# Layer 0's mixers in another order of steps, with other PSUM tiles, and the heads' norm as a product with a matrix of ones

## The chip, the core and the metric

The kernel runs on one core of a Trainium2 chip. The core has five engines with queues of their own that run at the same time: TensorE (PE: matrix products; PEld is its weight loading, which overlaps the products), VectorE (DVE), ScalarE (ACT), GpSimd (POOL) and SyncE (SP), which issues the loads of weights. Each engine takes its instructions in the order in which they stand in its queue; an instruction that has to wait for another engine holds back everything behind it. TensorE writes its results into PSUM, which has eight banks of 128 partitions by 512 fp32 numbers, and ScalarE or VectorE read them from there; a bank can be written again only when its readers are done. The metric is the device time of one execution in microseconds (us).

## What is computed (cut)

Two blocks on 512 positions of width 1024. Layer 0 of the first block has a mixer of two parts, a gated linear attention with four heads (GLA) and a sparse attention with eight heads (NSA); behind it come feed-forward layers, a spatial gating unit and a second block, which the change does not touch. Of layer 0's mixer:

```python
def _gla(q, k, v, g_lr, r, w_gate, b_gate, norm_g):
    glog = log_sigmoid(g_lr @ w_gate + b_gate) / 16          # the decays, (512, 4 heads x 64)
    b = cumsum of glog within chunks of 64 positions
    q_t, k_t, k_end = qc * exp(b), kc * exp(-b), kc * exp(b_last - b)
    a = where(causal, q_t @ k_t.T, 0)                        # within a chunk
    S_t = exp(b_last) * S_(t-1) + k_end.T @ v                # from chunk to chunk
    o = a @ v + q_t @ S_prev
    o = o * rsqrt(mean(o * o, axis=-1) + 1e-6) * norm_g      # each head's norm, over its 128 features
    return o * silu(r)

def _nsa(q, kc, vc, ks, vs, kw, vw, gate_logits, ...):
    k_cmp, v_cmp = compress(kc), compress(vc)                # 31 blocks of the 512 positions
    p_c = masked_softmax(q @ k_cmp.T);  o_c = p_c @ v_cmp
    # here every block is selected and the window is the whole sequence: both are causal attention
    o_s = masked_softmax(q @ ks.T) @ vs
    o_w = masked_softmax(q @ kw.T) @ vw
    return g0 * o_c + g1 * o_s + g2 * o_w

m = concatenate([_gla(...), _nsa(...)]) @ w_out
```

## The kernel before, in words

Matrix products with weights are done in split precision. `unit` loads 128x1024 weights (`wraw`), ScalarE rounds them to `whi` (line 272) and VectorE takes the rest `wlo` (line 273); `split` does the same with activations (lines 280 and 281). `mm3` then makes three products (lines 286 to 288). So one projection of 512 positions and 1024 inputs is 24 products with 512 columns each; here it is called a projection.

Layer 0's mixer is not written as one loop. Its parts are generators, and a string, `SEQUENCE`, is walked letter by letter: each letter takes the next step of a part. The letters are:

- `A`: scores of one head and branch (`sn`, `halves`: q k for four blocks of 128 queries, causal mask added by a product), their row maximum on VectorE (`mx`, line 934), exponentials with row sums on ScalarE (`pn`, line 936), and the division and gate on GpSimd (line 941). There are 16 such steps (8 heads, 2 branches).
- `T`: the 10 transposes of these probabilities (`pt`, `halves`, line 960) and their split into `pth` and `ptl` (lines 280 and 281).
- `P`: the products with the values (`on`, line 975); after every second one VectorE adds the result into `ob` (line 983).
- `c`: the compressed scores and softmax of one block of 128 queries (`sc`, line 873; lines 877 to 891), four steps.
- `C`: the transposes of the compressed probabilities (`ptc`, line 898), their split, and the products with the compressed values (`oc`, lines 286 to 288), copied to `ob` by ScalarE (line 905).
- `g`: the next step of the GLA part, in the order of `steps` in `gla`: two projections `gk`, the decays, two projections `gq`, and then `decayed` and the four projections `gv` by turns, `states`, and four projections `gr`. `decays` is a small transpose (`glrp`), a copy (`glrT`), two products (`zg`), and for each of two halves a log sigmoid and a running sum (lines 1007 to 1011 and 1054). `decayed` makes `e1` and from it the end-decayed keys, transposes these (`ktp`, line 1067) and scales `gq` and `gk`.
- `0` to `3`: the four GLA heads, four steps each: `atp`, `gop`, then the norm (`gsum`, `grc`, `cbg`), and the product with the gate (`goh`). `s`: the splits of `ob`.

A scheduler places the instructions of these steps on each engine near the place where the letters stand, not exactly there. PSUM banks are tiles with tags: in layer 0 tag `g` has two banks and serves projections, `sc`, `ptc`, `oc`, `glrp`, `zg`, `ktp` and the heads; tags `x` and `y` have one bank each and serve the transposes of `T` and, ahead of them, `kcp` and `vcp` (the compressed keys and values, line 803); `a`, `b` and `c` serve the scores; `o` the values.

After layer 0's mixer the output projection starts (`l`, `first_half("eo", ...)`), which reads the heads and `ob` from `cat`.

The program of the kernel before around the change:

Of the kernel before, what the change touches and what calls it, by code (L numbers as in the profile page):

```python
# [10 lines left out]
F32 = mybir.dt.float32  # L11
# [3 lines left out]
AF = mybir.ActivationFunctionType  # L15
# [4 lines left out]
P = 128  # L20
T = 512
NT = 4
# [3 lines left out]
EPS = 1e-6  # L26
# [180 lines left out]
for _k, _v in VEC_SIZES.items():  # L207
# [6 lines left out]

SEQUENCE = ("Acgc Acgcg CT AgTgP ATgP AgTP AgTgP ATgP ATgP AgTPg ATgP0 A0TgP0 AT1P1 ATgP12 AT2P2 ATgP03 A1T3Ps2 sT3P s3Ps"
            .replace(" ", ""))

RINGS = (("raw", 3), ("hi", 4), ("lo", 4)), (("raw", 2), ("hi", 2), ("lo", 2))  # L220
# [17 lines left out]
class Kernel:  # L238
# [395 lines left out]
    def run(self):  # L634
        tc, nc, a = self.tc, self.nc, self.a
        with ExitStack() as ctx:
            def pool(name, bufs=1, **kw):
                return ctx.enter_context(tc.tile_pool(name=name, bufs=bufs, **kw))

            cp = pool("const")  # L640
            self.small = pool("small", 2)
            self.rbp = pool("rbp", 1)
            self.rings = {r: [pool("w" + r, n)] * n for r, n in RINGS[0]}
            self.A = pool("A", 2)

            nc.scalar.preload_act_table_set("natural_log_exp_and_others")
            self.vecs = cp.tile([P, NVEC], F32, name="vecs")
            nc.scalar.dma_start(self.vecs, a["vecs"][:, :NVEC])
            self.consts = cp.tile([P, NCONST], F32, name="consts")
            self.coff = self.a["coff"]  # L650
            self.ident = self.cst("ident")
            self.ones = cp.tile([P, P], F32, name="ones")
            nc.vector.memset(self.ones, 1.0)
            self.mhalf = cp.tile([P, NT], F32, name="mhalf")
            nc.vector.memset(self.mhalf, -0.5)
            self.identb = cp.tile([P, P], BF, name="identb")
            self.causb = cp.tile([P, P], BF, name="causb")
            self.mod = cp.tile([P, 48], F32, name="mod")

            cat = self.layer0_mix()  # L660
            self.ps = pool("ps", 2, space=PSUM, reuse_waits="tile")
            self.pbufs = {"g": 2, "o": 2, "s": 4}
            self.wide = True
            for r, n in RINGS[1]:
                self.rings[r] = self.rings[r] + [pool(f"w{r}2", n, reuse_waits="tile")] * n
            self.hp = pool("hp", reuse_waits="tile")
            self.mp = pool("mp", reuse_waits="tile")
            self.B = pool("B", 2, reuse_waits="tile")
            self.rows = pool("rows", reuse_waits="tile")
            self.h = self.hp.tile([P, NT, D], F32, name="h")  # L670
            nc.scalar.dma_start(self.h, a["x"])
            st, evac = self.norm_evac(self.tokens(), "ng01", False)
            tail = self.first_half("eo", cat, evac)
            tail, st = self.ffn(0, tail, st)
            tail, st = self.sgu(tail, st)
            tail, st = self.ffn(1, tail, st)
            tail, st = self.mixer2(tail, st)
            self.swiglu(tail, st)
            assert self.pos == len(self.plan)


    def layer0_mix(self):
        tc, nc, a = self.tc, self.nc, self.a
        with ExitStack() as ctx:
# [4 lines left out]
            nb = ctx.enter_context(tc.tile_pool(name="nsa", bufs=1))  # L689
# [121 lines left out]
            gb = ctx.enter_context(tc.tile_pool(name="gla", bufs=1, reuse_waits="tile"))  # L811
            gw = ctx.enter_context(tc.tile_pool(name="glw", bufs=2, reuse_waits="tile"))
            gla, heads = self.gla(x, col, rb, ntm, gb, gw)
            parts = dict(zip("cCATP", self.nsa_attention(qs, khh, klo, ntm, vhl, kc, vcmp, nb, wk, ob)))
            parts["g"] = gla
            parts.update(zip("0123", heads))

# [30 lines left out]
    def nsa_attention(self, qs, khh, klo, ntm, vhl, kc, vcmp, nb, wk, ob):  # L848
# [13 lines left out]
        def compressed():  # L862

            for i in range(NT):
                p = split_parts[i % 2]()[:, :256].bitcast(F32)
                pcs.append(p)
                p = p.rearrange("p (h c) -> p h c", h=8)
                neg = self.cst("cneg").rearrange("p (t c) -> p t c", t=NT)[:, i]
                msk = self.cst("cmask").rearrange("p (t c) -> p t c", t=NT)[:, i]
                for g in range(2):  # L870
                    s = self.bank(self.ps, "sc", "g")
                    for j in range(4):
                        nc.tensor.matmul(s[:, j * 64:(j + 1) * 64], qs[:, g, j, i * P:(i + 1) * P], kc[g], start=True, stop=True)

                    sp = s[:, :256].rearrange("p (h e c) -> p h e c", h=4, e=2)
                    pg = p[:, 4 * g:4 * g + 4]
                    nc.vector.tensor_tensor(pg, sp[:, :, 0], neg.unsqueeze(1).to_broadcast([P, 4, 32]), ALU.add)
                    nc.vector.tensor_tensor(pg, pg, sp[:, :, 1], ALU.add)
                mx = st.tile([P, 8], F32, tag="cmx", name="cmx", bufs=2)
                nc.vector.tensor_reduce(mx, p, AX.X, ALU.max)  # L880
                nc.gpsimd.tensor_tensor(p, p, mx.unsqueeze(2).to_broadcast([P, 8, 32]), ALU.subtract)
                nc.scalar.activation(p, p, AF.Exp)
                if i == 0:

                    nc.vector.tensor_tensor(p, p, msk.unsqueeze(1).to_broadcast([P, 8, 32]), ALU.mult)
                sm = st.tile([P, 8], F32, tag="csm", name="csm", bufs=2)
                nc.vector.tensor_reduce(sm, p, AX.X, ALU.add)
                nc.vector.tensor_scalar_max(sm, sm, 1e-30)
                nc.vector.reciprocal(sm, sm)
                nc.vector.tensor_tensor(sm, sm, g3[:, i, :, 0], ALU.mult)  # L890
                nc.gpsimd.tensor_tensor(p, p, sm.unsqueeze(2).to_broadcast([P, 8, 32]), ALU.mult)
                yield

        def compressed_values():
            for g in range(2):
                pt = self.bank(self.ps, "ptc", "g")
                for i in range(NT):
                    nc.tensor.transpose(pt[:, i * P:(i + 1) * P], pcs[i][:, g * P:(g + 1) * P], self.ident)
                ph, pl = (t() for t in split_parts)
                self.split(ph, pl, pt)  # L900
                v = [t[:, g].rearrange("p h d -> p (h d)") for t in vcmp]
                for e in range(2):
                    o = self.bank(self.ps, "oc", "g")
                    self.mm3(o, tuple(t[:, e * P:(e + 1) * P] for t in v), (ph, pl), True, True)
                    nc.scalar.copy(ob[:, 2 * g + e], o)
            yield

# [41 lines left out]
        def transpose_steps():  # L949
            for k in todo:  # L950
                ps = probs.pop(k)
                parts[k] = []
                for e, kbs in enumerate(((0,), (1, 3), (2,))):
                    n = 256 if e == 2 else T
                    pt = self.bank(self.ps, f"pt{e}_", "xy"[e]) if e < 2 else halves[:, 1]
                    for kb in kbs:
                        c0 = place[kb][1]
                        for i in range(kb, NT):
                            c = c0 + (i - kb) * P
                            nc.tensor.transpose(pt[:, c:c + P], ps[i][:, kb * P:(kb + 1) * P], self.ident)  # L960
                    ph, pl = (t() for t in split_parts)
                    self.split(ph[:, :n], pl[:, :n], pt)
                    parts[k].append((ph, pl))
                yield
# [18 lines left out]
                        nc.vector.tensor_tensor(t, t, o[half * 64:half * 64 + 64], ALU.add)  # L983
                yield

        return compressed(), compressed_values(), score_steps(), transpose_steps(), value_steps()

    def pv(self, o, p, nk, wk, v, eng, pt):

# [23 lines left out]
    def gla(self, x, col, rb, ntm, gb, wk):  # L1013
# [78 lines left out]
        def steps():  # L1092
            for i in range(2):
                nc.vector.tensor_mul(gk[:, i], self.fm("gk", x), rb)
                yield
            decays()
            yield
            queries(0)
            yield
            queries(1)  # L1100
            yield
            gv.append(gb.tile([P, NT, T], F32, tag="gv", name="gv"))
            tm = self.tm("gv", x, (2, 2, 2, 2), 512, pairs=((0,), (1,), (2,), (3,)))
# [24 lines left out]
        def head(h):  # L1128
# [17 lines left out]
            sq = wk.tile([P, T], F32, tag="a", name="gsq", bufs=1)  # L1146
            nc.scalar.activation(sq, o, AF.Square)
            yield
            gs = self.bank(self.ps, "gsum", "g")
            for c in range(NT):  # L1150
                nc.tensor.matmul(gs[:, c:c + 1], sq[:, c * P:(c + 1) * P], self.ones[:, 0:1],
                                 start=True, stop=True)
            rc = self.small.tile([P, NT], F32, tag="rcol4", name="grc", bufs=4)
            self.pow_half(rc, gs[:, :4], 1.0 / 128.0, EPS)
            yield
            o = self.bank(self.ps, "cbg", "g")
            self.col_to_bc(o, rc)
            t = wk.tile([P, T], F32, tag="b", name="goh")
            nc.vector.tensor_mul(t, g, o)
            if self.cat is None:  # L1160
                self.cat = self.pair(self.A)
            self.split(self.cat[0][:, h], self.cat[1][:, h], t)
# [695 lines left out]
```

## Time and profile before

| | |
|---|---|
| median of three runs | 2034.1 us (2033.73 to 2039.08) |
| the profiled execution, its own time | 2034.54 us |
| its span from first to last instruction | 2032.7 us |
| TensorE busy over the span | 97% |
| VectorE, ScalarE, GpSimd busy | 68%, 43%, 22% |
| layer 0's mixer, to its last product with values | about the first 271 us of the span |

TensorE is the busy engine of the whole, so time is saved where TensorE waits, where its granted clock is low, or where it has less to do. The places below are given in us from the start of the span.

### The profile page before, as it was taken

How to read it: one execution, taken by the hardware profiler on the slowest of the kernel's cores; microseconds unless marked ns; L12 is line 12 of the kernel's file. 1: busy time of each engine (PE TensorE's matmuls, PEld its weight loads, DVE VectorE, ACT ScalarE, POOL GpSimd, SP SyncE). 2: the span in 40 equal slices, each digit the busy share in tenths (PEclk: the TensorE clock that was granted, in tenths of full speed). 3: DMA queues.
4: the chain of work that ended last, by engine and by line, in shares of the span. 5: the costliest groups of instructions: out<-in, count | busy, mean ns of one | idle time of the engine just before them, and what ended most of it. 6: DMA issues, size and time to landing. Idle time of an engine off the chain costs nothing.

```text
span 2032.7 us, 26315 instructions
## 1 busy us (share of the span) xinstructions
PE 1981.8 (97%) x10120; PEld 1674.6 (82%) x10120; DVE 1385.0 (68%) x1896; ACT 882.4 (43%) x1466; POOL 454.2 (22%) x349
## 2 busy tenths in 40 slices
PE   8989999999999899999999999999999999999997
PEld 6867889888888788888988888898888889888885
DVE  7676555799995758886688996633563655545964
ACT  5445555544344434224634443434755333532432
POOL 3222223433402100003344330200000002222306
PEclk9989999999999999999999999999999999999998
DMA  7311132323331746652233333132122223323231
GB/s 253 89 32 43 42 135 91 107 83 114 104 115 62 277 154 193 204 182 79 94 94 104 104 113 109 61 103 73 61 72 67 83 94 94 104 73 125 84 94 42
DMA packets 60589, 213.56 MB, mean 105 GB/s; under 512 B 6951, under 2 KB 8296, under 8 KB 60080
## 3 DMA queue, kind: packets, MB, share of 16 engines
q1 hardware_dynamic: 57888, 203.89, 31.0%
q0 software_dynamic: 1328, 4.23, 0.7%
q10 hardware_dynamic: 1248, 3.76, 0.6%
q8 instruction: 80, 1.31, 0.3%
q14 instruction: 45, 0.37, 0.1%
HBM read 206.59 MB, written 2.10 MB: 103 GB/s over the span
## 4 chain that ended last, share of the span: by engine, by line
PE 82%; DVE 7%; issue 5%; POOL 4%; ACT 1%; DMA 0%; SPq 0%; POOLq 0%; ACTq 0%; DVEq 0%
PE g L286 12%; PE g L288 12%; PE g L287 12%; PE a L286 6%; PE a L287 6%; PE a L288 6%; PE t L286 2%; PE t L288 2%; PE t L287 2%; PE h L287 2%; PE h L288 2%; PE h L286 2%; PE l L286 2%; PE l L288 2%; PE l L287 2%
## 5 line engine op out<-in xcount | busy, mean ns | idle before, releaser
L273 DVE TENSOR_TENSOR wlo<-wraw,whi 128x1024 fp32r<-128x1024 f32 (+1 forms) x310 | 445.9, 1442 | 183.3 <-ACT whi L272 180.1
L272 ACT CAST whi<-wraw 128x1024 fp32r<-128x1024 f32 (+1 forms) x310 | 323.5, 1045 | 403.8 <-PE g L287 203.8
L286 PE MATMUL g<-a,whi 128*128 128x512 f32 x1200 | 473.7, 395 | 0.0
L288 PE MATMUL g<-a,wlo 128*128 128x512 f32 x1200 | 470.0, 392 | 0.0
L287 PE MATMUL g<-a,whi 128*128 128x512 f32 x1200 | 469.8, 391 | 0.0
L288 PEld LDWEIGHTS g<-a,wlo 128*128 128x128 f32 x1200 | 225.9, 188 | 46.8
L286 PEld LDWEIGHTS g<-a,whi 128*128 128x128 f32 x1200 | 226.3, 189 | 45.8 <-DVE a L1614 0.2
L287 PEld LDWEIGHTS g<-a,whi 128*128 128x128 f32 x1200 | 226.3, 189 | 45.0
L286 PE MATMUL a<-whi,a 128*128 128x512 f32 x624 | 243.3, 390 | 0.0
L288 PE MATMUL a<-whi,a 128*128 128x512 f32 x624 | 242.8, 389 | 0.0
L287 PE MATMUL a<-wlo,a 128*128 128x512 f32 x624 | 242.8, 389 | 0.0
L286 PEld LDWEIGHTS a<-whi,a 128*128 128x128 f32 x624 | 117.2, 188 | 24.5 <-DVE a L1768 0.2
L288 PEld LDWEIGHTS a<-whi,a 128*128 128x128 f32 x624 | 117.1, 188 | 24.5
L287 PEld LDWEIGHTS a<-wlo,a 128*128 128x128 f32 x624 | 117.2, 188 | 23.9
L273 DVE TENSOR_TENSOR wlo<-wt,whi 128x1024 fp32r<-128x1024 f32 x64 | 101.7, 1588 | 32.6 <-ACT whi L272 30.9
L1755 POOL TENSOR_TENSOR wt<-wraw,wraw 128x1024 f32<-128x1024 f32 x32 | 99.0, 3095 | 95.3 <-DMA wraw<-wbig 95.3
L561 POOL TENSOR_TENSOR mg<-a,rowng 128x512 f32<-128x512 f32 x28 | 38.7, 1388 | 342.6 <-DVE a L553 340.1
L286 PE MATMUL h<-a,whi 128*128 128x256 f32 x384 | 108.7, 286 | 2.0 <-ACT a L555 0.9
L280 ACT CAST a<-yt 128x512 fp32r<-128x512 f32 x64 | 39.9, 623 | 161.6 <-POOL yt L1755 117.1
L287 PE MATMUL h<-a,whi 128*128 128x256 f32 x384 | 108.4, 283 | 1.5 <-DVE a L614 1.5
L288 PE MATMUL h<-a,wlo 128*128 128x256 f32 x384 | 107.9, 283 | 0.0
L272 ACT CAST whi<-wt 128x1024 fp32r<-128x1024 f32 x64 | 67.1, 1048 | 72.2 <-PE g L287 60.5
(431 smaller groups left out, 3526.7 us busy)
## 6 DMA issues: line engine op xcount, KB each, us to landing
wraw<-wbig SPq DMA_DIRECT2D x320, 512.0 KB, 3.7
wada<-wada SPq DMA_DIRECT2D x48, 512.0 KB, 3.5
cw<-cmp_w SPq DMA_DIRECT2D x2, 1024.0 KB, 10.4
rowng<-rows POOLq DMA_DIRECT2D x4, 512.0 KB, 5.8
h<-x ACTq DMA_DIRECT2D x1, 2048.0 KB, 10.2
out<-a SPq DMA_DIRECT2D x8, 256.0 KB, 2.2
xin<-xT SPq DMA_DIRECT2D x3, 512.0 KB, 7.9
qt<-qt ACTq DMA_DIRECT2D x12, 128.0 KB, 2.3
```

The costliest lines, as they stand in the source:

```text
L272: self.nc.scalar.copy(hi, raw)
L273: self.nc.vector.tensor_tensor(lo, raw, hi.bitcast(F32), ALU.subtract)
L280: self.nc.scalar.copy(hi, src)
L286: mm(out, s[0], m[0], start=start, stop=False)
L287: mm(out, s[0], m[1], start=False, stop=False)
L288: self.gemm = mm(out, s[1], m[0], start=False, stop=stop).ins
L561: nc.gpsimd.tensor_tensor(mg[c], t, g[:, c * 512:c * 512 + 512], ALU.mult)
L1755: nc.gpsimd.tensor_tensor(t, a, b, op)
```

## The change

The order of the steps is another one, `C` is cut into two steps (`C` now stands for the transposes and their split, `D` for the products with the compressed values), the compressed scores and the transposes of the compressed probabilities take the PSUM banks of tags `x` and `y` instead of `g`, the decays come after the two projections `gq` and not before them, and a head's norm is made in another way: before, four products with one column of ones gave the sums as columns, VectorE and GpSimd made the factor (`pow_half`, with a power of -0.5 on GpSimd), and four products spread it over a bank (`col_to_bc`); now one product of a 128x128 matrix of ones with the squares gives the sum spread over the bank, and ScalarE makes the factor as exp(-0.5 ln(sum/128 + eps)).

```diff
-SEQUENCE = ("Acgc Acgcg CT AgTgP ATgP AgTP AgTgP ATgP ATgP AgTPg ATgP0 A0TgP0 AT1P1 ATgP12 AT2P2 ATgP03 A1T3Ps2 sT3P s3Ps"
+SEQUENCE = ("Acgcgcgc ACgDT AgTP AgTgP AgTP ATgP ATgP ATgP AgTPg ATgP0 A0TgP0 AT1P1 ATgP12 AT2P2 ATgP03 A1T3Ps2 sT3P s3Ps"
...
+            self.epsc = cp.tile([P, 1], F32, name="epsc")
+            nc.vector.memset(self.epsc, EPS)
...
-            parts = dict(zip("cCATP", self.nsa_attention(qs, khh, klo, ntm, vhl, kc, vcmp, nb, wk, ob)))
+            parts = dict(zip("cCDATP", self.nsa_attention(qs, khh, klo, ntm, vhl, kc, vcmp, nb, wk, ob)))
...
-                    s = self.bank(self.ps, "sc", "g")
+                    s = self.bank(self.ps, "sc", "xy"[g])
...
+        ptcs = []
+
+        def compressed_transposed():
+            for g in range(2):
+                pt = self.bank(self.ps, "ptc", "xy"[g])
+                for i in range(NT):
+                    nc.tensor.transpose(pt[:, i * P:(i + 1) * P], pcs[i][:, g * P:(g + 1) * P], self.ident)
+                ptcs.append(tuple(t() for t in split_parts))
+                self.split(*ptcs[g], pt)
+            yield
+
         def compressed_values():
             for g in range(2):
-                pt = self.bank(self.ps, "ptc", "g")
-                for i in range(NT):
-                    nc.tensor.transpose(pt[:, i * P:(i + 1) * P], pcs[i][:, g * P:(g + 1) * P], self.ident)
-                ph, pl = (t() for t in split_parts)
-                self.split(ph, pl, pt)
                 v = [t[:, g].rearrange("p h d -> p (h d)") for t in vcmp]
                 for e in range(2):
                     o = self.bank(self.ps, "oc", "g")
-                    self.mm3(o, tuple(t[:, e * P:(e + 1) * P] for t in v), (ph, pl), True, True)
+                    self.mm3(o, tuple(t[:, e * P:(e + 1) * P] for t in v), ptcs[g], True, True)
                     nc.scalar.copy(ob[:, 2 * g + e], o)
...
-            decays()
-            yield
             queries(0)
             yield
             queries(1)
+            yield
+            decays()
             yield
...
             gs = self.bank(self.ps, "gsum", "g")
-            for c in range(NT):
-                nc.tensor.matmul(gs[:, c:c + 1], sq[:, c * P:(c + 1) * P], self.ones[:, 0:1],
-                                 start=True, stop=True)
-            rc = self.small.tile([P, NT], F32, tag="rcol4", name="grc", bufs=4)
-            self.pow_half(rc, gs[:, :4], 1.0 / 128.0, EPS)
+            nc.tensor.matmul(gs, self.ones, sq, start=True, stop=True)
             yield
-            o = self.bank(self.ps, "cbg", "g")
-            self.col_to_bc(o, rc)
             t = wk.tile([P, T], F32, tag="b", name="goh")
-            nc.vector.tensor_mul(t, g, o)
+            nc.scalar.activation(t, gs, AF.Ln, bias=self.epsc, scale=1.0 / 128.0)
+            nc.scalar.activation(t, t, AF.Exp, scale=-0.5)
+            nc.vector.tensor_mul(t, g, t)
```

How this moves instructions, at three places.

The first place is TensorE's queue behind the scores of the first `A`. In the kernel before, the eight products of the first `c` (`sc`) are followed by the scores of the second `A` (`sn_12`, `halves`):

```order
L846 MATMUL sn_11_806<-klo_107,qs 128x128
L873 MATMUL sc_843<-kc_115,qs 128x64 x4
L873 MATMUL sc_850<-kc_116,qs 128x64 x4
L845 MATMUL sn_12_925<-khh_105,qs 128x512
L846 MATMUL sn_12_925<-klo_109,qs 128x512
L927 LDWEIGHTS identb
L927 MATMUL sn_12_925<-causb,identb 128x128
L845 MATMUL halves_804<-khh_105,qs 128x256
L846 MATMUL halves_804<-klo_109,qs 128x256
```

In the changed kernel the same place reads (line numbers are those of the changed kernel):

```order
L848 MATMUL sn_11_808<-klo_109,qs 128x128
L875 MATMUL sc_845<-kc_117,qs 128x64 x4
L286 MATMUL g_12_876<-a_100,whi_872 128x512
L287 MATMUL g_12_876<-a_101,whi_872 128x512
L288 MATMUL g_12_876<-a_100,wlo_873 128x512
```

The first projection `gk` now starts after four of the eight compressed scores; 16 of its 24 products stand ahead of the other four. All four projections `gk` and `gq` follow one another in this way with a `c` between them, and the second `A` stands behind the third of them, `gq`'s first; `gq`'s second one stands after it, between the transposes `ptc`.

The second place is VectorE's queue where the decays are made. Before, from the copy `glrT` on, the log sigmoids and running sums (`ls`, `bk`) stand between the last compressed softmax and the splits of `ptc`:

```order
L1049 COPY glrT<-glrp_1046 16x512
L880 TENSOR_REDUCE cmx<-ptl 128x8
L939 RECIPROCAL sums<-sums 128x2
L1007 TENSOR_SCALAR ls_1055<-zg_1052 128x512
L887 TENSOR_REDUCE csm<-ptl 128x8
L1008 SCALAR_TENSOR_TENSOR ls_1054<-ls_1055,zg_1052 128x512
L888 TENSOR_SCALAR csm<-csm 128x8
L889 RECIPROCAL csm<-csm 128x8
L890 TENSOR_TENSOR csm<-csm,gates 128x8
L1011 TENSOR_TENSOR bk<-ls_1055,ls_1054 128x512
L281 TENSOR_TENSOR ptl<-ptc_1072,pth 128x512
L1054 SCALAR_TENSOR_TENSOR bk<-reset,bk 128x512
```

Now they stand among the row maxima of the scores (`mx`) and the splits of `T` (`ptl<-pt`):

```order
L1057 COPY glrT<-glrp_1213 16x512
L947 RECIPROCAL sums<-sums 128x2
L942 TENSOR_REDUCE mx<-sn_15_1175 128x1
L281 TENSOR_TENSOR ptl<-pt_15_1239,pth 128x512
L947 RECIPROCAL sums<-sums 128x2
L1015 TENSOR_SCALAR ls_1222<-zg_1219 128x512
L281 TENSOR_TENSOR ptl<-pt_15_1248,pth 128x512
L1016 SCALAR_TENSOR_TENSOR ls_1221<-ls_1222,zg_1219 128x512
L281 TENSOR_TENSOR ptl<-halves_806,pth 128x256
L942 TENSOR_REDUCE mx<-sn_15_1272 128x1
L1019 TENSOR_TENSOR bk<-ls_1222,ls_1221 128x512
L942 TENSOR_REDUCE mx<-sn_15_1273 128x1
```

On TensorE no projection stands between `glrp` and the first `ktp` any more: the third and fourth `A`, the second and third `T`, the first and second `P`, then the fifth `A`, the fourth `T` and seven products of the third `P` stand there, and only behind `ktp` the first projection `gv`. Before, both projections `gq` stood in that stretch.

The third place is the end of ScalarE's queue for layer 0, the last head (`goh`) and the last `T` (`pt_23`, `halves`). Before:

```order
L1147 ACTIVATE gsq<-gop_2656 128x512
L280 CAST pth<-pt_23_2695 128x512
L280 CAST a_2576<-goh 128x512
L280 CAST pth<-pt_23_2704 128x512
L280 CAST pth<-halves_804 128x256
L671 DMA h<-x 128x4096
L280 CAST a_2576<-goh 128x512
```

Now the logarithm and the exponential of the last head stand ahead of the second cast of the last `T`:

```order
L280 CAST pth<-pt_23_2667 128x512
L280 CAST a_2554<-ob 128x512
L1162 ACTIVATE goh<-gsum_2691,epsc 128x512
L1163 ACTIVATE goh<-goh 128x512
L280 CAST pth<-pt_23_2676 128x512
L280 CAST pth<-halves_806 128x256
```

From the second `gv` projection to the heads, and after layer 0, the queues are in the same order as before, but for the instructions of the heads' norms.

## Rows read from the trace of the kernel before

**Rows 1.** Windows: PE, PEld, DVE, ACT, POOL busy us (instructions), PE clock, DMA share, GB/s.

```profile
84.51:91.34 6.83, 5.65 (x15) 4.66 (x16) 5.39 (x17) 2.73 (x9) 4.83 (x9) 0.50 0.17 52
...
111.82:125.47 13.65, 9.72 (x24) 5.90 (x23) 9.43 (x18) 7.00 (x14) 1.45 (x3) 0.50 0.00 0
...
215.00:272.00 57.00, 55.78 (x390) 50.16 (x389) 39.19 (x79) 30.30 (x74) 15.95 (x23) 1.00 0.13 39
```

**Rows 2.** Waits of PE from 78.84 to 162.5: us in total, times, longest.

```profile
PE halves L845 <- ACT pn L936: 2.5, 1, 2.5
```

**Rows 3.** Chain of waits: start, us on the chain, what.

```profile
89.17 0.43 PE g L287
...
105.10 0.23 PE g L286
...
141.83 0.44 PE ktp L1067 x4
...
162.42 0.25 PE t L288
```

**Rows 4.** Timeline: start, us, what; in brackets the idle time before.

```profile
80.71 1.03 PE L873 MATMUL sc<-kc,qs 128*128 128x64 f32 x8
...
86.10 0.30 DVE L281 TENSOR_TENSOR vcmp<-vcp,vcmp 32x128 fp32r<-32x128 f32 x1
```

**Rows 5.** Timeline of PE: one T, one A, and what follows.

```profile
150.95 1.04 PE L960 MATMUL pt<-consts,pn 128*128 128x128 f32 x8
...
153.26 0.44 PE L845 MATMUL sn<-khh,qs 128*128 128x512 f32 x1
...
154.98 0.62 PE L1067 MATMUL ktp<-consts,e 128*128 128x128 f32 x4
```

**Rows 6.** Groups of DVE from 78.84 to 162.5: busy us, mean ns, idle before.

```profile
L934 DVE TENSOR_REDUCE mx<-sn 128x1 f32<-128x512 f32 (+2 forms) x18 | 10.1, 568 | 0.9 <-PE sn L927 0.8
...
L281 DVE TENSOR_TENSOR ptl<-pt,pth 128x512 fp32r<-128x512 f32 x9 | 6.0, 686 | 0.8 <-ACT pth L280 0.8
...
L934 DVE TENSOR_REDUCE mx<-halves 128x1 f32<-128x256 f32 x6 | 2.5, 419 | 1.2 <-PE halves L927 1.2
L1054 DVE TENSOR_TENSOR_SCAN bk<-reset,bk 128x512 f32<-128x512 f32 x2 | 2.4, 1216 | 0.0
L939 DVE RECIPROCAL sums<-sums 128x2 f32<-128x2 f32 x12 | 1.9, 160 | 0.1
```

**Rows 7.** Timeline: the decays' first transposes, and the product ahead of `ktp`.

```profile
108.92 0.60 PE L1048 MATMUL glrp<-consts,ntm 128*16 128x128 f32 x4 [0.42 <-DVE ptl L878]
...
128.38 0.69 DVE L1064 TENSOR_TENSOR e<-e,gk 128x512 f32<-128x512 f32 x1
```

**Rows 8.** Timeline of POOL, two of its divisions.

```profile
143.04 2.44 POOL L941 TENSOR_SCALAR pn<-pn,sums,gates 128x512 f32<-128x512 f32 x4 [12.74 <-ACT pn L936]
148.78 3.79 POOL L941 TENSOR_SCALAR pn<-pn,sums,gates 128x512 f32<-128x512 f32 x4 [3.30 <-DVE sums L939]
```

**Rows 9.** Timeline of DVE beside the second of these divisions.

```profile
148.78 0.67 DVE L1073 TENSOR_TENSOR gq<-gq,e 64x512 f32<-64x512 f32 x1
...
149.65 0.99 DVE L1073 TENSOR_TENSOR gq<-gq,e 64x512 f32<-64x512 f32 x1
```

**Rows 10.** Windows of 215 to 272, tile `gsum` alone: PE, PEld and DVE busy.

```profile
215.00:272.00 57.00, 3.95 (x32) 3.96 (x32) 0.63 (x4) 1.00 0.13 39
```

**Rows 11.** The same for tile `cbg`.

```profile
215.00:272.00 57.00, 4.47 (x32) 3.88 (x32) 2.60 (x4) 1.00 0.13 39
```

**Rows 12.** Waits of PE from 215 to 272: us in total, times, longest.

```profile
PE cbg L460 <- POOL grc L455: 1.1, 1, 1.1
```

**Rows 13.** Chain of waits: one of the decays' two fp32 products of 128x512.

```profile
110.29 1.14 PE zg L1052 x2
```

**Rows 14.** Groups of ACT from 215 to 272.

```profile
L1121 ACT ACTIVATE sig<-sig,ones 128x512 f32<-128x512 f32 x3 | 2.2, 723 | 0.0
L1122 ACT ACTIVATE sig<-sig 128x512 f32<-128x512 f32 x3 | 1.9, 633 | 0.0
```

More of the change, by code (lines that the diff above doesn't have):

```diff
@@ L984, in value_steps @@
                 yield
-        return compressed(), compressed_values(), score_steps(), transpose_steps(), value_steps()
+        return compressed(), compressed_transposed(), compressed_values(), score_steps(), transpose_steps(), value_steps()
     def pv(self, o, p, nk, wk, v, eng, pt):
```

## The prediction, made before the run

> **What bounds the kernel now.** I read the windows first, because the table of times already says that TensorE is busy for 97% of the span: little is to be had from the other engines as such, and a place is worth looking at only where TensorE waits, runs at a low clock, or does work that the change takes away. The order of the instructions shows that layer 0's mixer is the same up to the second `A` (about 79 us) and again from the last product of the second `gv` projection on, which begins at 162.42 [rows 3], but for the heads' norms. [...] The chain of waits gives the prices: a product of 512 columns takes 0.43 us of the chain at the low clock and 0.23 at the high one [rows 3]. [...] In the last 57 us of the mixer TensorE is busy for 55.78 at full clock [rows 1]: there only less work counts. After it TensorE is the bound, so what layer 0 saves should reach the end in full.
>
> **The change part by part: the front.** It removes no product. I add up TensorE's queue from the first compressed scores, at 80.71 [rows 4], to the start of the third `A`, at full clock. Four steps `c` of 8 small products: 1.03 us each [rows 4], 4.1. Four projections: 24 x 0.23 = 5.5 each [rows 3], 22.1. The second `A`: 1.7, as a later one takes from 153.26 to 154.98 [rows 5]. One `T`: 1.0, most of it the eight `pt` with 1.04, whose ends overlap the next [rows 5]. Eight transposes of the compressed probabilities, like those eight: 0.9. Twelve products `oc`: 12 x 0.23 = 2.8. The sum is 32.6, so 113.3.
>
> To that come two waits. First, `sc` now takes banks `x` and `y`, and `y` holds `vcp` until its last split on VectorE, which starts at 86.10 and takes 0.30 [rows 4]. The 4 + 16 products ahead of the second half of the first `c` end at about 80.71 + 0.5 + 16 x 0.23 = 84.9, so TensorE waits 1.5 us, to 86.4. Second, the last transposes and the two `oc` banks, copied away by ScalarE, wait for each other in part; in the old place these and the decays idled for 3.9 [rows 1], and with a projection among them I take 1.0. So the third `A` starts at 115.8, and its first row maximum, behind two products of 512 columns and the mask, at about 117.2. The old 2.5 us wait [rows 2] goes, because projections now stand where the exponentials are made.
>
> **The middle.** From there the `decays` stand among the third to fifth `A`, with no projection behind which their chain could hide: the first `gv` projection is queued behind the first `ktp`. I price VectorE's queue to the last product ahead of `ktp`. Two `A`: each 3 x 0.568 + 0.419 + 2 x 0.160 = 2.44 [rows 6], 4.9. Two `T`: two splits of 0.686 [rows 6] and one of 0.41, 3.6 together. A full pass over 128x512 costs 0.69 whatever it does [rows 6, 7]; the copy `glrT`, `ls` and `bk` of two halves (3 passes and a running sum of 1.216 [rows 6], 3.27 each), two additions to `ob`, and four passes for `e`, two scalings of `gq` and the product come to 0.7 + 6.5 + 1.4 + 2.9 = 11.5. Together 19.9, so 137.1. One us more for its waits on ScalarE's exponentials and logarithms, and one for GpSimd: `ktp` starts at about 139. As a cross-check, before it took from 108.92 to 128.38 + 0.69 [rows 7], 20.2 us, for the same decays with other neighbours.
>
> That last microsecond I take from two rows. GpSimd's four divisions took 2.44 us beside little and 3.79 beside two scalings of `gq` [rows 8], and one of these took 0.99 where its twin took 0.67 [rows 9]: 0.31 more, for an instruction with two operands in SBUF. Eight such stand ahead of `ktp`; in the old place GpSimd was busy for only 1.45 us of the 13.65 [rows 1], now its divisions run beside. Eight times 0.31 is 2.5; not all will meet, so 1.0, with 0 and 2.5 as bounds. [...]
>
> **The end of the stretch.** Behind 139 TensorE has `ktp` at the low clock, twice its 0.44 [rows 3], 0.9, as this middle is as sparse as the old one was at 111.82. Then the first `gv` projection, of which some 5 us go at 0.43 a product and the rest at 0.23, 7.8; the second `ktp` 0.5, an `A` 1.7, a `T` 1.0, and the second `gv` 5.5. These 17.4 us end at 156.4. The chain ends the old one at 162.42 + 0.25 [rows 3], some 0.2 behind the pace of 0.23 at which products follow one another and by which I counted, so I take 162.5: a gain of 6.1.
>
> **The heads.** Removed are four `gsum` and four `cbg`, busy for 3.95 [rows 10] and 4.47 us [rows 11], on the chain about 3.5 and 4.0 as their ends overlap, and the one wait for `grc`, 1.1 [rows 12]: 8.6. Added are four fp32 products of 128x512. The nearest row is one of `zg`, 1.14 [rows 13], with fewer partitions; if it holds, 4.6. They may be paced closer, at 0.9, since 1.14 holds a start; then 3.6. So 4.0 to 5.0, and I take 4.5. ScalarE gets a logarithm and an exponential per head, 0.72 and 0.63 by their likes [rows 14], 5.4 us beside 30.30 busy of 57 [rows 1], which I cost at nothing in the middle heads: products of other heads stand behind. If that cover is gone they cost 1.35 each. VectorE loses the spread's reading of a bank, which it was not waited for.
>
> The sum: 6.1 + 4.5 = 10.6, and 2034.54 - 10.6 = 2023.9, say 2024. The profiled execution stands 0.4 above the median of 2034.1, which is nothing beside the bounds. With GpSimd at 0, no `oc` wait, and the first `gv` wholly at full clock (2.3 less), the front and middle give 10.4 and the heads 5.0: 2019. With twice the waits (+3) and 1.5 more at GpSimd, and a `gv` wholly at half clock (+2.5), the heads at 4.0, the gain is 3: 2031. This is the likeliest case's own range.
>
> **The rivals.** *ScalarE in the last head.* The logarithm and the exponential of the last head stand ahead of the casts of the last `T`, for whose products TensorE waits. If that happens at each head, it costs 4 x 1.35 = 5.4, the heads give -0.9 and the total is 5.2: 2029.3. Against it: ScalarE is idle for nearly half of these 57 us [rows 1]. At the last head alone it is 1.35, inside the range. Chance 0.13.
>
> *The clock falls again in the front.* If the 1.5 us for bank `y` brings what the 2.5 us wait brought, 5.65 busy at half clock lose 2.8, and some 2 more go in the `oc` stretch: 2028.7. For it: the old spell began right behind such a wait [rows 1, 2]. Chance 0.15.
>
> *VectorE and GpSimd block each other in full.* A GpSimd division alone is 2.44/4 = 0.6, beside VectorE 0.95 [rows 8]. If each of the eight instructions waits for one, 8 x 0.87 (0.95 less a little) = 7 us in place of 1.0: 2030. Half of them would give 2026.5. [...] Against it: one of two scalings in [rows 9] was not late at all. Chance 0.08.
>
> *The other side: the decays' chain takes as long as before.* From `glrp` at 108.92 [rows 7] to `ktp` at 141.83 [rows 3] were 32.9 us. With `glrp` at about 117.5 `ktp` would come at 150.4, the stretch end at 167.8, 5.1 to 5.3 late, and less 4.5 at the heads the kernel takes 2035.3. It breaks even with `ktp` at 149.6 and is slower by over 0.3% from 155.7. Against it: the product was done at 129.07 and `ktp` only stood in TensorE's queue behind the two `gq` projections. Chance 0.12, a third of it beyond 155.7.
>
> *Nothing moves,* as the waits were hidden: against it, half-clock spells of TensorE itself are hidden by nothing. Within the last rival's lower part.
>
> **How the numbers follow.** The likeliest has 0.52, its time is 2024. The other cases reach 2028.7 to 2035.3; the range from 2018.5 to 2031 leaves out the last one (0.12) and some of the ends, 2 in 10. What a measurement of this kernel can tell from no change is about 0.3%, 6.1 us, so faster begins at 2028. The likeliest case is nearly all below; of the clock's, ScalarE's and GpSimd's rivals somewhat under a half: 0.67 faster. Slower needs `ktp` beyond 155.7, or 150 with other misses: 0.08. Within 0.3% is the rest, 0.25.
>
> **What would show it.** Right: no low clock at 84, a wait of `sc` for the split of `vcmp` of about 1.5 us; `glrp` near 118, `ktp` near 139, the last product of the second `gv` near 156; `gsum` as four products of 0.9 to 1.14 us, no `cbg` and no `grc`; `l` some 10 us earlier than before. Wrong: `ktp` at 149.6 or later, casts `pth` behind `goh` on ScalarE with TensorE waiting for them, a clock of 0.50 through the projections, or a first `gv` that runs wholly at 0.43 a product.

## The result and the profile after

The changed kernel takes 2023.16 us (median of 4 runs, 2022.9 to 2024.86), the kernel before 2034.49 beside it: a ratio of 0.994, 95% interval 0.9928 to 0.9952. That is 11.3 us less, more than the 6.1 us that the prediction called measurable; 2024 was forecast. The span of the profiled execution fell from 2032.7 to 2021.5.

I read it by two stretches of TensorE's queue: from the first compressed scores (80.71 in both) to the end of the second `gv` projection, which holds the same work before and after, and from there to `l`, which differs by the heads' norm alone. The windows of the kernel before (columns: PE, PEld, DVE, ACT, POOL busy us with instructions, PE clock, DMA share, GB/s):

```profile
80.71:162.50 81.79, 71.38 (x349) 55.80 (x348) 57.83 (x129) 37.03 (x92) 25.28 (x39) 0.87 0.13 39
162.50:271.31 108.81, 105.04 (x728) 90.78 (x726) 75.01 (x157) 59.87 (x147) 30.23 (x45) 1.00 0.14 44
```

The same stretches of the changed kernel, and its two spells at low clock:

```profile
80.71:154.88 74.17, 66.84 (x349) 53.79 (x348) 58.05 (x129) 36.61 (x92) 27.63 (x39) 0.93 0.14 43
154.88:260.31 105.43, 101.17 (x671) 84.87 (x670) 74.60 (x153) 63.21 (x155) 26.82 (x41) 1.00 0.16 51
...
87.13:90.54 3.41, 3.41 (x11) 2.64 (x10) 2.02 (x4) 0.30 (x1) 2.58 (x4) 0.50 0.30 74
131.50:138.33 6.83, 4.68 (x20) 3.75 (x19) 4.84 (x9) 2.49 (x7) 3.45 (x2) 0.50 0.00 1
```

The first stretch is 7.62 us shorter, the second 3.38, 11.0 together. In the first, the 349 products are the same; TensorE is busy for 4.54 us less, because half as much time is left at 0.50 (10.2 us, before 20.5 by [rows 1]), and idle for 7.33 in place of 10.41. In the second it is busy for 3.87 us less and idle for 0.49 more.

The waits of TensorE from 78 to 160 in the changed kernel (us in total, times, longest):

```profile
PE pt L968 <- POOL pn L949: 2.1, 2, 1.6
PE sc L875 <- DVE vcmp L281: 1.5, 1, 1.5
PE ptc L902 <- POOL ptl L893: 1.3, 1, 1.3
PE halves L968 <- ACT pn L944: 1.2, 1, 1.2
PE pt L968 <- DVE ptl L281: 0.7, 1, 0.7
PE sn L847 <- ACT pn L944: 0.5, 1, 0.5
```

The 2.5 us for the exponentials of the second `A` [rows 2] are gone, and the 1.5 us for `vcp` have come. The marks of the prediction in TensorE's timeline of the changed kernel (start, us, what; in brackets the idle time before):

```profile
86.55 0.60 PE L875 MATMUL sc<-kc,qs 128*128 128x64 f32 x4 [1.52 <-DVE vcmp L281]
...
117.79 0.47 PE L847 MATMUL sn<-khh,qs 128*128 128x512 f32 x1
...
119.66 0.60 PE L1056 MATMUL glrp<-consts,ntm 128*16 128x128 f32 x4
...
138.93 0.62 PE L1075 MATMUL ktp<-consts,e 128*128 128x128 f32 x4
139.30 0.48 PE L286 MATMUL t<-whi,a 128*128 128x512 f32 x1
...
154.64 0.40 PE L288 MATMUL t<-whi,a 128*128 128x512 f32 x1
```

In the chain that ends in `ktp` stands a wait for GpSimd. In the timelines of POOL and DVE the divisions of the blocks of 256 and 128 columns took 0.98 us in the second `A`, with VectorE idle or nearly so, and 3.45 in the fourth:

```profile
111.64 0.98 POOL L949 TENSOR_SCALAR pn<-pn,sums,gates 128x256 f32<-128x256 f32 x2
...
131.65 3.45 POOL L949 TENSOR_SCALAR pn<-pn,sums,gates 128x256 f32<-128x256 f32 x2 [0.97 <-DVE sums L947]
```

```profile
132.05 0.68 DVE L1019 TENSOR_TENSOR bk<-ls,ls 128x512 f32<-128x512 f32 x1
...
132.99 1.21 DVE L1062 TENSOR_TENSOR_SCAN bk<-reset,bk 128x512 f32<-128x512 f32 x1
134.12 0.66 DVE L1070 TENSOR_TENSOR e<-bk 128x512 f32<-128x512 f32 x1
```

The excess is 2.47 us, the three VectorE instructions with both operands in SBUF that ran meanwhile took 0.68 + 1.21 + 0.66 = 2.55, and none of them was late or long (the other `bk` of its kind took 0.68, the other running sum 1.22, the other `e` 0.68). Here GpSimd alone paid: by the profile, whose starts on GpSimd are rough, the first division began 0.40 us ahead of the first of the three and took 1.34 us, its like in the second `A` 0.55. By what mechanism it was held is not shown. Behind the divisions stand the transposes `pt`, behind these a cast on ScalarE, and behind the cast, in ScalarE's queue, the exponentials `e` on which VectorE then waits (a line of TensorE's timeline, two of ScalarE's, one of VectorE's waits):

```profile
135.16 1.75 PE L968 MATMUL pt<-consts,pn 128*128 128x128 f32 x7 [1.63 <-POOL pn L949]
```

```profile
136.31 0.58 ACT L280 CAST pth<-pt 128x512 fp32r<-128x512 f32 x1 [4.34 <-PE pt L968]
136.79 0.63 ACT L1078 ACTIVATE e<-bk 128x512 f32<-128x512 f32 x1
```

```profile
DVE gq L1081 <- ACT e L1078: 2.0, 1, 2.0
```

At the heads, the products of the new norm (window of the second stretch, tile `gsum` alone: PE, PEld, ACT busy), and the wait that is new:

```profile
154.88:260.31 105.43, 4.24 (x8) 1.28 (x8) 2.71 (x4) 1.00 0.16 51
```

```profile
255.28 0.66 PE L968 MATMUL pt<-consts,pn 128*128 128x128 f32 x4 [1.22 <-POOL pn L949]
255.78 1.02 PE L1159 MATMUL gsum<-gsq,ones 128*128 128x512 f32 x2
```

Four products of 1.06 us busy, 4.24, stand in place of 3.95 + 4.47 [rows 10, 11]. The wait for `grc` [rows 12] is gone; but before the last `T` a `cbg` stood ahead of the transposes, and without it they come 1.22 us too early for GpSimd's last division.

### The profile page after: what moved, and what is told of

It is laid out like the page before. It is cut to its first block, busy times and chain, and to the rows that moved or that the text cites. A ratio compares the mean times of both kernels' runs of the same rounds, so it can differ in the third digit from the quotient of the medians.

```text
span 2021.5 us, 26196 instructions
## 1 busy us (share of the span) xinstructions
PE 1973.2 (98%) x10064; PEld 1666.4 (82%) x10064; DVE 1384.3 (68%) x1893; ACT 885.3 (44%) x1474; POOL 452.0 (22%) x345
## 4 chain that ended last, share of the span: by engine, by line
PE 82%; DVE 7%; issue 5%; POOL 5%; ACT 1%; DMA 0%; SPq 0%; POOLq 0%; ACTq 0%; DVEq 0%
PE g L288 12%; PE g L286 12%; PE g L287 12%; PE a L287 6%; PE a L286 6%; PE a L288 6%; PE t L286 2%; PE h L287 2%; PE h L288 2%; PE h L286 2%; PE t L287 2%; PE t L288 2%; PE l L286 2%; PE l L288 2%; PE l L287 2%
```

## The experiments

All times beside the kernel before on the same chip (2034.3 to 2034.6 us). As the runs of one kernel lie 1 to 6 us apart, I read the edits above all by the stretches of one profile each: S1 from the first `sc` to the start of the second `gv`'s last product (before 81.55, changed 73.93), S2 from there to `l` (before 109.05, changed 105.67).

**The two halves.** `order_only` is the changed kernel with the old norm; `heads_only` the kernel before with the new one.

> The changed kernel with the old norm of the heads (columns of sums, GpSimd's power, spread over a bank). Theory: the two parts of the change add up. The last product of the second gv projection then ends near 154.9 us as in the changed kernel, the heads take what they took before, and the time is about 7.6 us below the kernel before, 2026.9. Rival: the parts depend on each other (the old heads stand in other places once the order moves), then it lies by more than 1.5 us beside 2026.9.

> The kernel before with the new norm of the heads alone. Theory: TensorE saves about 4.2 us of products and the wait of 1.1 us for GpSimd's power, but loses 1.2 us where the last cbg had covered GpSimd's last division, so 3.3 us in all, 2031.2. The prediction's term was 4.5, 2030.0. Rival: the logarithm and the exponential on ScalarE hold up the casts at each head, 5.4 us, and the time is 2035 or more.

Measured: 2025.59 us (ratio 0.9947, 0.9932 to 0.9962), S1 72.35, S2 109.00; and 2031.2 (0.9978, 0.9967 to 0.9988), S1 81.24, S2 105.70. In the stretches the parts add up: S2 hangs on the norm (3.35 us less in the old order of steps, 3.33 in the new), S1 on the order and the banks. ScalarE does not hold the heads up. S1 of `order_only` is 1.6 us shorter than that of the changed kernel with the same queue: its clock did not fall behind the wait for `vcp`.

```profile
86.20:89.61 3.41, 3.34 (x21) 3.02 (x22) 3.34 (x8) 1.00 (x1) 3.20 (x5) 1.00 0.19 29
```

So this execution (2024.83 us, the shortest of its four) lies below 2026.9 by the clock above all and not by the sum.

**Banks without the order, order without the banks.** `banks_g` puts `sc` and `ptc` of the changed kernel back on tag `g`:

```diff
-s = self.bank(self.ps, "sc", "xy"[g])
+s = self.bank(self.ps, "sc", "g")
...
-pt = self.bank(self.ps, "ptc", "xy"[g])
+pt = self.bank(self.ps, "ptc", "g")
```

> The changed order and the new norm, but the compressed scores and the transposes of their probabilities in the banks of tag g, as in the kernel before. Measured from the first compressed scores to the first product of the output projection (changed kernel 179.6 us, 177.7 without the low clock behind the wait for vcp, which two of the other runs don't show). Theory: the other banks are what lets the projections run ahead of the compressed scores; back in g each projection waits for the softmax of a c and each c for the projection's reader, so TensorE waits about 1 us at each of four places and the stretch takes 181 to 184 us, the whole 2025 to 2028. Rival: the order of the steps alone does it, and the stretch stays at 178 to 180, 2023.

`banks_only` makes the opposite edit, `"g"` to `"xy"[g]` in both lines, in the kernel before.

> The kernel before with one thing changed: the compressed scores and the transposes of their probabilities in the banks of tags x and y; old order of steps, old norm of the heads. The changed kernel with the banks of tag g took 12 us more than with x and y, all of its gain. Theory: the two belong together; in the old order the banks give a part, since the first projection can then start behind four compressed scores, but the stretch behind the compressed values has the same chain: from the first compressed scores to the last product of the second gv projection 76 to 79 us against 81.6 of the kernel before and 73.9 of the changed one, the whole 2029 to 2032. Rival: the banks do it all, 72 to 75 us and 2025 to 2027; or nothing in this order, 81 to 82 us, 2034.

Measured: `banks_g` 2035.07 us (0.9999, 0.999 to 1.0008), S1 86.50; `banks_only` 2027.46 (0.9963, 0.995 to 0.9976), S1 75.98. The new order with the old banks loses all that was won, 12.6 us in S1, more than I had expected, and is there 5.0 longer than the kernel before: the waits of the kernel before come back and longer ones with them, and 23.9 us of S1 run at 0.50, against 10.2 in the changed kernel (waits of PE in its first stretch):

```profile
PE ptc L902 <- POOL ptl L893: 3.3, 1, 3.3
PE halves L847 <- ACT pn L944: 2.5, 1, 2.5
PE sn L847 <- ACT pn L944: 2.5, 2, 1.9
PE pt L968 <- POOL pn L949: 1.5, 1, 1.5
PE g L286 <- DVE ptl L281: 1.2, 1, 1.2
```

The banks alone give 5.6 of the 7.6 us, at the short end of what the theory gave S1 (76 to 79 us; the time is below its 2029 to 2032). The order is worth something only with them: 2.0 more in the changed kernel, whose clock falls for 3.41 us behind the wait for `vcp` as that of `banks_only` does, and 3.6 in `order_only`, whose clock does not. Which part `sc` and which `ptc` has in this is not shown, as both lines were moved together.

**The wait for `vcp`.** `sc_bank_o` puts the second half of `sc` in the bank of tag `o`:

```diff
-s = self.bank(self.ps, "sc", "xy"[g])
+s = self.bank(self.ps, "sc", "xo"[g])
```

> The changed kernel with the second half of each compressed score in the bank of tag o, free until the first product with values, in place of y, which vcp still holds. Theory: the wait of 1.5 us for the split of vcp goes, and with it the low clock behind it, in which 8 products took 0.43 in place of 0.23 us: 1.5 + 1.6 = 3.1 us, 2020.0. Rival: the front is given back, at the wait for GpSimd's last compressed probabilities or because the decays' chain on VectorE decides anyway: 2023.

Measured: 2022.89 us (0.9937, 0.9922 to 0.9952), S1 71.97. Against the changed kernel S1 is 1.96 shorter, but 1.6 of that `order_only` has too, without the edit. Only 0.4 is the edit's: in place of 1.5 us for `vcp` TensorE waits 0.9 for the softmax's reading of the other bank. Up to `glrp` it wins 0.7 (36.66 us from the first `sc`, against 37.36 in `order_only`); 0.3 of that goes again behind it. The time is the rival's.

```profile
PE sc L875 <- DVE pth L880: 0.9, 1, 0.9
```

**GpSimd's long divisions.** `div_on_dve` gives the two of the fourth `A` to VectorE:

```diff
-nc.gpsimd.tensor_scalar(ps[k], ...)
+(nc.vector if (h, b) == (1, 1) and k < 2 else nc.gpsimd).tensor_scalar(ps[k], ...)
```

> The changed kernel with the last two divisions (blocks of 256 and 128 columns) of the fourth A on VectorE in place of GpSimd. In the changed kernel they take 3.45 us on GpSimd, beside two-operand instructions of VectorE, against 0.98 us for the same two earlier, and the transposes behind them wait. Theory: that block costs what it seems to, the transposes come 2 to 2.5 us earlier, ktp too, and the time is about 2021.0. Rival: ktp is bound by VectorE's own queue, into which the two divisions now go: the time stays at 2023 or rises by up to 0.7.

Measured: 2023.13 us (0.9931, 0.9917 to 0.9946), S1 73.83. From `glrp` to `ktp` it takes 17.87 us, against 19.27: the two on GpSimd did hold `ktp`, by 1.4 and not by the 2 to 2.5 that I had expected. What `ktp` waits for now is VectorE's own queue, as the rival had it:

```profile
135.82 1.11 PE L1075 MATMUL ktp<-consts,e 128*128 128x128 f32 x4 [1.19 <-DVE e L1072]
```

Nothing is kept against `order_only`'s 72.35, the profile with the same clock in front: the scheduler, too, moved `ktp` ahead of the products with values, and the low clock lasted for 10.24 us, so that the first `gv` began at the lower level.

```profile
131.06:141.30 10.24, 8.43 (x26) 6.59 (x27) 9.96 (x19) 5.30 (x15) 1.11 (x2) 0.50 0.00 0
```

**The last division.** `last_div_on_dve` has the same edit with `(h, b) == (7, 1)` and all four blocks.

> The changed kernel with the four divisions of the last A on VectorE in place of GpSimd. Theory: TensorE waits 1.2 us for them in the last T, where the last cbg of the kernel before had covered them; on VectorE they take a shorter time, the wait goes, and the time from the last product of the second gv projection to the output projection falls from 105.7 to 104.5 us, the prediction's term for the heads. The whole gains 1.2, at the edge of what rounds can tell. Rival: VectorE's queue puts the splits and the goh of that head later, and TensorE waits as long for them.

Measured: 2025.74 us (0.995, 0.9932 to 0.9967), S2 106.54, 0.9 longer. The rival holds: VectorE has the divisions in its queue, and TensorE waits 0.9 us for them in place of 1.2, and 1.0 in place of 0.3 for the additions to `ob`.

```profile
PE on L983 <- DVE ob L991: 1.0, 2, 0.7
PE pt L968 <- DVE pn L949: 0.9, 1, 0.9
```

**ScalarE's work in the norm.** `no_ln_exp` leaves the two activations out and multiplies with the sum in PSUM.

> The changed kernel without the logarithm and the exponential of the heads' norm: the gate is multiplied with the sum as it stands in PSUM, so the norm is left out. Theory: ScalarE's 5.4 us are hidden behind other products, and the time from the last product of the second gv projection to the output projection stays at 105.7 us, within 0.4. Rival: they hold up the casts of the last T steps, and it falls by 1.4 to 5.4 us.

Measured: 2022.73 us (0.9937, 0.9922 to 0.9952), S2 104.97: 0.7 less, not 5.4 and somewhat more than nothing. The 0.7 can't be put down to the two activations alone: without them the scheduler puts the last head's `gsum` ahead of the last `pt`, which changes the waits there (0.67 for `gsq` and 0.34 for GpSimd in place of 1.22).

**Where the decays stand.** The decays behind both `gq` projections are the weak place: TensorE's second spell of low clock and half of its idle time (3.9 of 7.3 us) lie between `glrp` and `ktp`. `decays_between_queries` puts them between the two, `decays_first` ahead of both, as in the kernel before, with all else of the change (here `decays_first`):

```diff
-            queries(0)
-            yield
-            queries(1)
-            yield
             decays()
             yield
+            queries(0)
+            yield
+            queries(1)
+            yield
```

> The changed kernel with the decays between the two projections gq in place of behind both, so that the second gq stands among the A and T steps behind the decays. Theory: TensorE's waits of some 4 us between glrp and ktp and the low clock there (131.5 to 138.3) come from having no projection in that stretch; with one there the stretch from the first compressed scores to the output projection falls from 177.7 to 173 to 175 us, the time to 2018 to 2020. Rival: the decays' chain on VectorE decides, TensorE's waits only move ahead of gq, and the stretch stays at 177 to 180, 2022 to 2024.

> The changed kernel with the decays ahead of both projections gq, as in the kernel before; new order of the letters, new banks, new norm. Theory: what helped with the decays between the projections (no low clock from 130 on, fewer waits) is cover behind them, so with both gq behind them it is as good: 175 to 177 us from the first compressed scores to the output projection, 2019 to 2022. Rival: with fewer projections in front the compressed softmax has no cover, TensorE waits there and its clock falls near 105: 178 us or more, 2023 or more.

Measured: 2020.67 us (0.9929, 0.9911 to 0.9947), S1 69.77; and 2016.44 (0.9912, 0.9895 to 0.9928), S1 66.85. From the first `sc` to `l` these are 175.5 us, at the theory's edge, and 172.5, better than the theory's 175 to 177. The second is the best version: 18 us below the kernel before and 7 below the changed one. Its profiled execution is the shortest of its four (2013.09 us, the others 2016.34 to 2017.63). In it the first stretch runs at full clock throughout, and the waits are half of the changed kernel's:

```profile
80.50:147.58 67.08, 63.58 (x348) 51.08 (x348) 57.58 (x129) 36.77 (x92) 28.48 (x39) 1.00 0.15 48
```

```profile
PE sc L875 <- DVE vcmp L281: 1.5, 1, 1.5
PE ptc L902 <- POOL ptl L893: 0.5, 1, 0.5
PE halves L847 <- DVE ptl L281: 0.5, 1, 0.5
PE pt L968 <- POOL pn L949: 0.5, 1, 0.5
PE halves L968 <- ACT pn L944: 0.3, 1, 0.3
```

From `glrp` to `ktp` it takes 29.10 us, 10 more than in the changed kernel, and that costs nothing, as two projections stand behind it: the product that `ktp` transposes was done at 119.26, and `ktp` came at 124.99, when TensorE's queue got there. Both were tried with the bank of tag `o` as well.

> The decays between the two projections gq, and the second half of each compressed score in the bank of tag o. Theory: the 1.5 us for vcp go as in the run with the bank alone, of which 0.7 was kept, so the stretch falls from 175.5 to about 174.8 us and by up to 2 more where the low clock at 109.6 doesn't come: 173 to 175, 2018.5 to 2020.5. Rival: the wait only moves to the softmax of the compressed scores, and the stretch stays at 175.5 to 177.

> The decays ahead of both projections gq (2016.4 in the run with that alone, 172.6 us from the first compressed scores to the output projection, with no low clock in between) and the second half of each compressed score in the bank of tag o. Theory: the 1.5 us for vcp become 0.9 for the softmax, 0.6 to 0.7 us are kept: 172 us, and the time is within what can be told of 2016. Rival: the shorter wait changes where the clock falls, and the stretch takes 174 us or more.

Measured: 2019.54 us (0.9923, 0.9908 to 0.9938), S1 70.67; and 2018.76 (0.9922, 0.9905 to 0.994), S1 67.32. Neither stretch is shorter than without the edit (69.77 and 66.85), so the bank `o` is no gain that could be seen. But each of these two profiles has 3.41 us more at low clock in S1 than its partner, 6.83 against 3.41 and 3.41 against none (windows of the two):

```profile
107.88:114.71 6.83, 6.83 (x22) 4.44 (x21) 4.75 (x7) 2.67 (x5) 2.97 (x4) 0.50 0.28 77
```

```profile
100.51:103.92 3.41, 3.41 (x12) 2.83 (x11) 3.41 (x11) 2.73 (x6) 1.61 (x2) 0.50 0.01 5
```

Up to `glrp`, ahead of these spells, the edit wins 0.7 us in both, as in `sc_bank_o` (23.36 against 24.09, and 14.68 against 15.39). Whether the shorter wait brings the low clock, as the rival of the second run says, or the two met by chance is not shown.

## Why the prediction was right

**The total** was right (10.6 us forecast, 11.2 in the span), by terms that were off in both directions; that they cancelled is luck.

**The front** came out 2.0 us late: the third `A` at 117.8 in place of 115.8. The wait for bank `y` was 1.52 us, as worked out. The 1.0 for the transposes and `oc` was 1.3, all of it for GpSimd's last compressed probabilities. What I had left to a rival is the rest: the clock fell behind the wait for 3.41 us, and 8 products at 0.43 cost 1.6, a third of the rival's 2.8 + 2. `order_only` and `decays_first` show the same wait without it.

**The middle** was right in its end (`ktp` 139 forecast, 138.93) by luck and not in its composition: it began 1.9 late and took 2.1 less. From the first row maximum it took 19.8 us where I had summed 21.9, but the window of these 19.82 us has VectorE, which I took for the bound, busy for 16.68:

```profile
119.11:138.93 19.82, 15.95 (x89) 12.10 (x88) 16.68 (x34) 11.85 (x32) 7.25 (x8) 0.83 0.02 6
```

The durations of its 34 instructions add up to 19.7 by the groups, close to my 19.9, but the start of one lies some 0.08 ahead of the end of the one before, which a sum of durations counts twice, and the last one ends 0.56 behind the window. The 3.1 us left are waits, 2.0 of them for the exponentials behind the long divisions. I had the right pair of engines in the last microsecond and charged the wrong one: VectorE kept its durations, GpSimd's two divisions took 3.45 us in place of 0.98. `div_on_dve` puts what reached `ktp` at 1.4, where I had taken 1.0.

**The end** was mis-sized: the first `gv` took 5.6 us and not 7.8, as the clock was back at 138.33, before it began; `ktp` too ran at the higher level. The `A` and `T` before the second `gv` held 0.66 of waiting. So 154.9 in place of 156.4, 7.6 us of gain against 6.1.

**The heads** gave 3.4, not 4.5. The price of the products was right (1.06 busy each, between 0.9, an estimate that no row shows, and the 1.14 of `zg`). The heads' term is off by the cover: I priced the removed `cbg` without asking what was being made behind it, and the last one had hidden GpSimd's division. Ln and Exp, taken at nothing, did not show as waits: in the changed kernel's S2 TensorE waits for no cast `pth`, and `no_ln_exp` without them is 0.7 shorter, in a queue that is not quite the same.

**The rivals.** The decays' chain as long as before: it was 19.3 us against 32.8. In `decays_first` it is 29.1 again, of which 5.7 are `ktp` standing in TensorE's queue with its input ready, and harmless, as projections fill it; the prediction's argument against this rival was right. ScalarE in the heads: against it stand `heads_only`, at 2031.2 and not 2035 or more, and `no_ln_exp`. VectorE and GpSimd blocking each other in full: beside the three instructions above GpSimd alone was longer, by 2.47 us, and nowhere else in the middle, so not the rival's 7. What I did not see is that the step which I priced as a cost, taking the projections from behind the decays, was a loss of 5.5 to 7 us inside the change: `decays_first` has the other parts' gain without it. Its S1 of 66.85 is 7.1 below that of the changed kernel and 5.5 below that of `order_only`, whose clock did not fall in the front either.

## What to carry to other kernels

A projection that waits for nobody is cover, and the place for it is behind the start of the longest chain, not ahead of it. Look at which PSUM banks let it run ahead before changing the order: here the banks carried most of the changed kernel's gain in the first stretch, and the order without them lost it all. When work is removed from the bound engine, ask what others were finishing behind it.

## What the runs showed of the hardware

In eight profiles TensorE's queue is the same from the first `sc` up to a wait of 1.5 us for `vcp`, which ends at 86.3 to 86.7. Behind it TensorE ran on at full clock in `order_only`, `div_on_dve`, `decays_between_queries` and `decays_first`; its clock fell to 0.50 for 3.41 us in the changed kernel, `no_ln_exp` and `banks_only`, and for 6.82 in `last_div_on_dve`:

```profile
87.68:94.50 6.82, 6.82 (x22) 5.67 (x21) 5.31 (x16) 1.36 (x2) 2.45 (x5) 0.50 0.48 132
```

Where the order is the same, from the first `sc` to `glrp` that is 37.36, 38.95 and 40.56 us, so 0, 1.6 or 3.2 us for the same instructions. What sets the moment at which the clock falls is not shown. Of executions that were only timed there is the mean granted clock of the whole span alone: for the four of `decays_first` it is 0.996, 0.995, 0.995 and 0.994 at spans of 2011.2, 2014.5, 2014.7 and 2015.8 us. How much of the scatter of the times the clock makes in all stays open.
